# A hybrid RWKV-7 / S5 layer: the w_ada column sums as matmuls, and triangular inverses built from 16-blocks

## Chip, cores, metric

The kernel runs on one core of a Trainium2 chip. The metric is the device time of one execution in microseconds (us), lower is better. Engines are named as in the profile: PE (TensorE matmuls), PEld (its weight loads), DVE (VectorE), ACT (ScalarE), POOL (GpSimd), SP (the engine whose queue issues nearly all DMAs).

## The reference

One layer on a sequence of 1024 tokens with 1024 features, all in float32. What matters here:

```python
c_act = jax.nn.silu(c)                       # c: (1, 1024)
ada = c_act @ w_ada[l] + b_ada[l]            # w_ada: (1024, 6144), 24 MB
sh_m, sc_m, g_m, sh_f, sc_f, g_f = jnp.split(ada, 6, axis=-1)
h = modulate(rms_norm(x), sh_m, sc_m)        # parts 0 and 1 of ada
proj = h @ w_in[l]
...                                          # RWKV-7 time mixing (8 heads) and S5 state space
x = x + g_m * mix                            # part 2
h = modulate(rms_norm(x), sh_f, sc_f)        # parts 3 and 4
x = x + g_f * ffn                            # part 5
```

The RWKV recurrence `S = S * w_t + sa b_t + v_t k_t` is computed in chunks of 64 tokens. Each chunk and head needs the inverse of a unit triangular 64x64 matrix; with 1024 tokens (16 chunks) and 8 heads there are 128 such matrices.

## The kernel before

The program is a set of Python generators that are woven together; from what they yield, the framework's scheduler orders each engine's instructions by a simulated time line (`schedule_with_timeline_sim=True` at the launch), and allots tile buffers and PSUM banks. On the chip each engine then works its own queue in that order.

**The w_ada sums.** `ada_load` (L280) loads a slab of w_ada for one part and `n` column blocks of 128 in four DMAs on SP's queue; each fills a tile `wada` [128, 2, 128n]. `ada_acc` (L289) makes `acc` [128, 128n]: eight terms, w_ada rows times the column `cact[:, k]` of silu(c), added up on DVE (L295, L297), or, where `eng` is not DVE, scaled on ACT (L299) and added on POOL (L300). `ada_cols` (L303) sums `acc` over the partitions with one matmul per column block against a column of ones (tile `pac`, L306) and adds the bias into `mod` (L307). Parts 0 and 1 are done in the start (L538 to L566) with n=4, two loads of both parts; parts 2 and 3 by `ada_steps` (L826) as `adg` (L1250) beside the end of the chunk chains and the S5 gate (`s5_glu`); parts 4 and 5 as `adl` (L1428) beside the first half of the output projection. These steps have n=2 and four `wada` buffers, so one step's load waits for the one before to be read. `adg` gives the steps j=0 and j=4 of each part to ACT and POOL. The PSUM tile of `ada_cols` comes from `ps_s` in `adg` and from `ps_a` in `adl`, banks that the S5 gate and the preparation of the chunks use as well.

**The inverses.** The sequence is worked in four quarters `qt` of 256 tokens; each has 32 matrices. `amats` (L953) writes the chunk matrices to `ak`; `l_write` (L984) puts the 64x64 triangles in DRAM (`l_d`). `solve` (L991) loads the two 32x32 diagonal blocks of each matrix with one row of `LU` per partition (64 matrices, split in two column halves over 128 partitions), and runs forward substitution over 31 columns, two instructions per column (L1006, L1008), on DVE for quarters 0 and 1 and on POOL for 2 and 3. The inverse X and its transpose VT go through DRAM (`x_d`, L1010, L1011) and come back in matmul layout (`XB`, `VB`, L1020, L1021). `rest` (L1013) builds the off-diagonal 32x32 block from two rounds of 32 small matmuls (`pG`, L1028; `pO`, L1038) with an ACT copy between, and writes the result over `ak`. The chunk chains (`chunk`, L1048) of that quarter need it.

**Order around it.** Quarters 0 and 1 run beside the S5 units and the z projection (`zhalf`). Quarters 2 and 3 are the generator `late` (L1421), which runs `alongside` the first half of the FFN `f0` (L1442): matmuls of the FFN (`mm3`, L270) fill TensorE between its steps. PSUM banks come from `ps_t` by tag; `ps_g` has one bank "g" and, in part of the program, a second one "G".

Of the kernel before, what the change touches and what calls it, by code (L numbers as in the profile page):

```python
# [9 lines left out]
F32 = mybir.dt.float32  # L10
# [7 lines left out]
P = 128  # L18
D = 1024
T = 1024  # L20
HT = 512
# [8 lines left out]
def kernel(  # L30
# [127 lines left out]
    for b in range(4):  # L158
        V.memset(rm[32 * b:32 * b + 32, b % 2:b % 2 + 1], 1.0)
    m01 = const.tile([P, HT], F32, name="m01")  # L160
# [52 lines left out]
    def col(name, i=0, n=1):  # L213
        gi, o = off[name]
        return cols[:, gi, o + i:o + i + n]

    cact = const.tile([P, 8], F32, name="cact")
    nkk = const.tile([P, 4], F32, name="nkk")
# [22 lines left out]
    x_d = dram.tile([4, 2, 65536], F32, name="x_d")  # L241
# [47 lines left out]
    def ada_acc(pl, wts, n, eng=V):  # L289

        acc = pl.tile([P, 128 * n], F32, tag="acc", bufs=2 if n > 2 else 3, name="acc")
        for k in range(8):
            wt = wts[k // 2][:, k % 2, :]
            if k == 0:
                V.tensor_scalar_mul(acc, wt, cact[:, 0:1])  # L295
            elif eng is V:
                V.scalar_tensor_tensor(out=acc, in0=wt, scalar=cact[:, k:k + 1], in1=acc, op0=ALU.mult, op1=ALU.add)  # L297
            else:
                S.mul(wt, wt, cact[:, k:k + 1])  # L299
                G.tensor_tensor(out=acc, in0=acc, in1=wt, op=ALU.add)  # L300
        return acc
# [16 lines left out]
    V.tensor_mul(cact, cact, col("c", 0, 8))  # L318
    def load_x(hf):
# [220 lines left out]
    acs = [ada_acc(sp, w, 4) for w in wa]  # L540
# [12 lines left out]
    acs = [ada_acc(sp, w, 4) for w in wa]  # L553
# [122 lines left out]

    s5_params(*s5q)
# [148 lines left out]
    def ada_steps(pl, parts, ps, mix=lambda j: j % 4):  # L826

        todo = []
        def cols():
            acc, part, j = todo.pop(0)  # L830
            ada_cols(acc, part, j, 2, ps("pac2")[:, 0:2])
        for part in parts:
            for j in (0, 2, 4, 6):
                todo.append((ada_acc(pl, ada_load(pl, part, j, 2, 4), 2, V if mix(j) else None), part, j))
                if len(todo) > 2:
                    cols()
                yield
        while todo:
            cols()
            yield  # L840
# [150 lines left out]
    def solve(qt):  # L991

        t_ = lambda nm, sh: RP[0].tile(sh, F32, tag=nm, name=nm)
        LU, tmp = t_("LU", [P, 32, 32]), t_("stmp", [P, 256])
        X, VT = (RP[0].tile([P, HT], F32, tag=nm, name=nm) for nm in ("XU", "VT"))
        X, VT = X.rearrange("p (i k) -> p i k", k=16), VT.rearrange("p (k i) -> p k i", i=32)
        for o in range(2):
            nc.sync.dma_start(LU[64 * o:64 * o + 64], l_d[qt][:, 0:2048].rearrange("r (i t) -> r i t", t=64)[:, :, 0:32])
        G.memset(X, 0.0)
        for o in range(2):  # L1000
            G.memset(X[64 * o:64 * o + 64].rearrange("p i k -> p (i k)")[:, 16 * o:512:33], 1.0)
# [7 lines left out]
        SOLVE.tensor_copy(VT.rearrange("p k i -> p i k"), X)  # L1009
        nc.sync.dma_start(x_d[qt, 0].rearrange("(r n) -> r n", r=P), X.rearrange("p i k -> p (i k)"))  # L1010
        nc.sync.dma_start(x_d[qt, 1].rearrange("(r n) -> r n", r=P), VT.rearrange("p k i -> p (k i)"))  # L1011

    def rest(qt):  # L1013

        XB, VB, GT = (t.rearrange("p (u k) -> p u k", k=32) for t in
                      [RP[0].tile([P, HT], F32, tag=nm, name=nm) for nm in ("XU", "VT")] + [tr("GT")])

        for o in range(2):
            src = x_d[qt, :, 32768 * o:32768 * o + 32768]
            nc.sync.dma_start(XB[:, :, 16 * o:16 * o + 16], src[0].rearrange("(u p k) -> p u k", u=16, k=16))  # L1020
            nc.sync.dma_start(VB[o::2], src[1].rearrange("(u p i) -> p u i", u=16, i=32))  # L1021
        aks = [sts[qt, q]["ak"] for q in range(2)]
# [7 lines left out]
        for h2 in range(2):  # L1030
            p0 = 64 * h2 + 32
            S.copy(GT[p0:p0 + 32].rearrange("p u (k o) -> p u o k", o=2),
                   ps[p0:p0 + 32].rearrange("p u (o k) -> p u o k", o=2))
# [394 lines left out]
    adl = ada_steps(pool("adp3", stack=das, side="right"), (4, 5), ps_a, lambda j: True)  # L1428
# [62 lines left out]
```

## Time and profile before

| | us |
|---|---|
| median of 3 runs | 1596.32 |
| lowest and highest run | 1594.2, 1597.29 |
| the profiled execution | 1596.48 |
| its span, first to last instruction | 1594.8 |

| engine | busy us | share of the span |
|---|---|---|
| PE | 1419.0 | 89% |
| PEld | 1143.2 | 72% |
| DVE | 929.3 | 58% |
| ACT | 562.7 | 35% |
| POOL | 519.8 | 33% |

All durations below are of the profiled execution, in us from the start of its span. A busy share is a mean over stages with different limits; PEclk is the clock that TensorE was granted, as a share of 2.4 GHz, and a record is one instruction in the trace. One float32 matmul of the program leaves two records. In a row of a time line, the bracket at the end is the idle time of the engine just before the row and what ended it.

### The profile page before, as it was taken

The page shows a single profiled execution, that of the slowest core. Times are in us where ns is not written, and L with a number is a line of the kernel's source. Part 1 is how long each engine was busy: PE and PEld are TensorE (multiplying, and loading weights), DVE is VectorE, ACT ScalarE, POOL GpSimd, SP SyncE. Part 2 cuts the span into 40 slices and gives each one's busy share as a digit, 9 for nine tenths or more (in the row PEclk, how much of TensorE's full clock was granted, in tenths as well). Part 3 has the DMA queues.
Part 4 walks back from the last instruction along what each step waited for, and adds up shares of the span by engine and source line. Part 5 has one row for each costly group of instructions (what it writes and reads, how often), then busy time and mean ns, then how long its engine had stood idle before and what let it go on. Part 6 is the DMA issues. An engine that isn't in the chain of part 4 may idle for free.

```text
span 1594.8 us, 23226 instructions
## 1 busy us (share of the span) xinstructions
PE 1419.0 (89%) x9167; PEld 1143.2 (72%) x9167; DVE 929.3 (58%) x1618; ACT 562.7 (35%) x909; POOL 519.8 (33%) x480
## 2 busy tenths in 40 slices
PE   3897888988968847989999998999997999999997
PEld 3675666776856535777777776778886888888885
DVE  5968328688656899464467655446356533333335
ACT  4442244443345632242145223224444222222223
POOL 4358333222143415163000007000611244444543
PEclk9998899899979869899999999899998999999999
DMA  9447895563664477244233243315621423232331
GB/s 286 139 139 244 264 328 193 164 163 110 154 160 125 126 219 217 59 103 97 61 99 91 88 106 89 84 54 167 177 80 40 151 87 106 92 106 92 98 101 53
DMA packets 255692, 211.80 MB, mean 133 GB/s; under 512 B 71894, under 2 KB 223072, under 8 KB 252000
## 3 DMA queue, kind: packets, MB, share of 16 engines
q1 hardware_dynamic: 254096, 208.67, 44.0%
q8 instruction: 72, 1.18, 0.3%
q0 software_dynamic: 816, 0.57, 0.2%
q10 hardware_dynamic: 672, 1.08, 0.2%
q14 instruction: 36, 0.29, 0.1%
HBM read 166.54 MB, written 45.84 MB: 133 GB/s over the span
## 4 chain that ended last, share of the span: by engine, by line
PE 51%; DVE 19%; DMA 13%; POOL 5%; ACT 5%; issue 4%; SPq 2%; DVEq 0%; ACTq 0%; POOLq 0%
PE pdn L270 11%; PE pgate L270 10%; PE pup L270 10%; PE pz L270 5%; PE po L1314 4%; DMA wada<-in_w_ada_dram 3%; PE pu L367 2%; DMA rawd<-in_ffn_w_down_dram 2%; PE p L1062 2%; DVE acc L297 2%; POOL stmp L1006 2%; POOL XU L1008 2%; PE pY L762 1%; PE pA L962 1%; DMA LU<-l_d 1%
## 5 line engine op out<-in xcount | busy, mean ns | idle before, releaser
L270 PE MATMUL pdn<-wd,act 128*128 128x512 f32 x1056 | 271.7, 398 | 1.4 <-DVE x L1363 0.5
L270 PE MATMUL pup<-h,hl_up 128*128 128x512 f32 x1056 | 266.5, 395 | 0.2 <-ACT hl_up L131 0.2
L270 PE MATMUL pgate<-h,hl_g 128*128 128x512 f32 x1056 | 262.7, 394 | 2.1 <-ACT hl_g L131 2.0
L270 PEld LDWEIGHTS pdn<-wd,act 128*128 128x128 f32 x1056 | 197.3, 189 | 49.1 <-DVE x L1363 2.4
L270 PEld LDWEIGHTS pgate<-h,hl_g 128*128 128x128 f32 x1056 | 196.6, 188 | 47.2 <-issue 3.2
L270 PEld LDWEIGHTS pup<-h,hl_up 128*128 128x128 f32 x1056 | 197.5, 188 | 43.9 <-issue 2.1
L270 PE MATMUL pz<-hT,hl_z 128*128 128x256 f32 (+1 forms) x1008 | 192.6, 347 | 35.0 <-ACT zo L872 13.5
L1363 DVE TENSOR_TENSOR x<-pdn,x 128x512 f32<-128x512 f32 x176 | 118.8, 688 | 176.6 <-PE pdn L270 176.4
L270 PEld LDWEIGHTS pz<-hT,hl_z 128*128 128x128 f32 x1008 | 159.0, 206 | 64.8 <-ACT zo L872 18.2
L1398 DVE TENSOR_TENSOR rawd<-rawd,gfb 128x1024 f32<-128x1024 f32 x44 | 57.2, 1300 | 111.5 <-DMA rawd<-in_ffn_w_down_dram 89.9
L1314 PE MATMUL po<-wo,yhl 128*128 128x512 f32 x384 | 98.7, 410 | 9.0 <-ACT yhl L1299 4.2
L1314 PEld LDWEIGHTS po<-wo,yhl 128*128 128x128 f32 x384 | 74.4, 197 | 27.3 <-ACT yhl L1299 4.3
L131 ACT CAST wd<-rawd 128x1024 fp32r<-128x1024 f32 x44 | 45.6, 1051 | 122.1 <-DVE rawd L1398 88.8
L131 ACT CAST hl_up<-raw_up 128x1024 fp32r<-128x1024 f32 x44 | 46.2, 1051 | 114.6 <-PE pup L270 105.1
L297 DVE SCALAR_TENSOR_TENSOR acc<-wada,cact,acc 128x256 f32<-128x256 f32 (+1 forms) x112 | 79.0, 710 | 6.9 <-DMA wada<-in_w_ada_dram 5.3
L875 POOL TENSOR_TENSOR zo<-zo,zm 128x512 f32<-128x512 f32 x28 | 44.2, 1580 | 99.5 <-ACT zo L872 86.6
L127 POOL TENSOR_TENSOR hl_g<-raw_g,hl_g 128x1024 fp32r<-128x1024 f32 x19 | 45.5, 2394 | 78.7 <-ACT hl_g L131 78.7
L127 POOL TENSOR_TENSOR yhl<-yt,yhl 128x512 fp32r<-128x512 f32 x16 | 25.0, 1562 | 135.5 <-ACT yhl L1299 130.9
L1392 ACT ACTIVATE sgt<-pgate 128x512 f32<-128x512 f32 x44 | 26.3, 599 | 121.0 <-PE pgate L270 120.0
L127 POOL TENSOR_TENSOR wd<-rawd,wd 128x1024 fp32r<-128x1024 f32 x19 | 49.7, 2616 | 57.4 <-ACT wd L131 57.4
L127 POOL TENSOR_TENSOR wo<-wraw,wo 128x512 fp32r<-128x512 f32 x32 | 44.4, 1393 | 73.6 <-ACT wo L131 73.6
L127 POOL TENSOR_TENSOR hl_up<-raw_up,hl_up 128x1024 fp32r<-128x1024 f32 x19 | 49.9, 2628 | 50.0 <-ACT hl_up L131 50.0
(373 smaller groups left out, 2345.5 us busy)
## 6 DMA issues: line engine op xcount, KB each, us to landing
raw_g<-in_ffn_w_gate_dram SPq DMA_DIRECT2D x44, 512.0 KB, 4.0
raw_up<-in_ffn_w_up_dram SPq DMA_DIRECT2D x44, 512.0 KB, 3.9
rawd<-in_ffn_w_down_dram SPq DMA_DIRECT2D x44, 512.0 KB, 3.6
wada<-in_w_ada_dram SPq DMA_DIRECT2D x64, 256.0 KB, 3.2
zw_d<-hl_z SPq DMA_DIRECT2D x14, 1024.0 KB
hl_z<-zw_d SPq DMA_DIRECT2D x14, 1024.0 KB, 4.9
wada<-in_w_ada_dram SPq DMA_DIRECT2D x16, 512.0 KB, 7.8
wraw<-in_w_out_dram SPq DMA_DIRECT2D x32, 256.0 KB, 4.4
```

Of the source, the lines that this page charges most:

```text
L127: (eng or G).tensor_tensor(out=out, in0=a, in1=b, op=ALU.subtract)
L131: S.copy(dst[:, 0], src)
L270: PE.matmul(ps, lhsT=lf(a, k), rhs=rf(b, k), start=(n == 0), stop=(n == 3 * kb - 1))
L297: V.scalar_tensor_tensor(out=acc, in0=wt, scalar=cact[:, k:k + 1], in1=acc, op0=ALU.mult, op1=ALU.add)
L367: PE.matmul(pu[hf, b], lhsT=uw[b][:, a_, k, :], rhs=hT[hf, k][:, b_, :], start=(k == 0 and n == 0), stop=(k == 7 and n == 2))
L875: G.tensor_tensor(out=o, in0=o, in1=zm[:, 0:HT], op=ALU.add)
L1006: SOLVE.tensor_tensor(out=t, in0=LU[:, j, j + 1:32].unsqueeze(2).to_broadcast([P, nt, nk]), in1=X[:, j:j + 1, 0:nk].to_broadcast([P, nt, n ...
L1008: SOLVE.tensor_tensor(out=X[:, j + 1:32, 0:nk], in0=X[:, j + 1:32, 0:nk], in1=t, op=ALU.add)
L1062: PE.matmul(ps[r, h], lhsT=a, rhs=b, start=(n == 0), stop=(n == len(ops) - 1))
L1314: PE.matmul(pss[i], lhsT=yh[k][:, a, 128 * i:128 * i + 128], rhs=wo[:, b], start=(k == 4 and n == 0), stop=(k == 3 and n == 2))
L1363: V.tensor_tensor(out=t, in0=ps, in1=t, op=ALU.add)
L1398: V.tensor_tensor(out=raw, in0=raw, in1=gfb, op=ALU.mult)
```

## The change

Two edits come together.

1. `ada_acc` makes its sums on TensorE. A tile `cz` [128, 8, 32] is zero but for column 0 of each k, which is silu(c). For each k one matmul has `cz[:, k, :]` (128 rows, 32 columns) as the stationary side and the w_ada slab as the moving side; k modulo 4 chooses one of four column groups of the array, so four sums run in four groups of 32 output partitions, in two rounds. ACT copies the PSUM tile `pada` to `acc`; `ada_cols` is unchanged. `ada_steps` loads with eight `wada` buffers instead of four, one step ahead of the sum. `acc` has two buffers. The DVE form and the ACT and POOL form go.
2. `solve` substitutes only in the 16x16 diagonal blocks (128 of them, one per partition): 15 columns, 30 instructions, on DVE for every quarter. `rest` then builds each 32x32 diagonal inverse by three rounds of 64 matmuls of 32x32 (`pH`, `pX`, `pV`), each followed by a DVE operation of 128x512, before the two old rounds. `x_d` is one buffer for all quarters, zeroed once by two DMAs on POOL's queue.

```diff
-    def ada_acc(pl, wts, n, eng=V):
-        acc = pl.tile([P, 128 * n], F32, tag="acc", bufs=2 if n > 2 else 3, name="acc")
+    def ada_acc(pl, wts, n, ps):
         for k in range(8):
-            wt = wts[k // 2][:, k % 2, :]
-            if k == 0:
-                V.tensor_scalar_mul(acc, wt, cact[:, 0:1])
-            elif eng is V:
-                V.scalar_tensor_tensor(out=acc, in0=wt, scalar=cact[:, k:k + 1], in1=acc, op0=ALU.mult, op1=ALU.add)
-            else:
-                S.mul(wt, wt, cact[:, k:k + 1])
-                G.tensor_tensor(out=acc, in0=acc, in1=wt, op=ALU.add)
+            g = slice(32 * (k % 4), 32 * (k % 4) + 32)
+            PE.matmul(ps[g, 0:128 * n], lhsT=cz[:, k, :], rhs=wts[k // 2][:, k % 2, :], start=(k < 4), stop=(k > 3),
+                      tile_position=(0, 32 * (k % 4)))
+        acc = pl.tile([P, 128 * n], F32, tag="acc", bufs=2, name="acc")
+        S.copy(acc, ps[:, 0:128 * n])
         return acc
...
-    acs = [ada_acc(sp, w, 4) for w in wa]
+    acs = [ada_acc(sp, w, 4, pst.tile([P, 512], F32, tag="tp", bufs=3, name="pada")) for w in wa]
...
+    def ada_steps(pl, parts, ps):
+        loads, todo = [], []
+        def acc():
+            w, part, j = loads.pop(0)
+            todo.append((ada_acc(pl, w, 2, ps("pada")), part, j))
...
+                loads.append((ada_load(pl, part, j, 2, 8), part, j))
+                if len(todo) > 0:
+                    cols()
+                if len(loads) > 1:
+                    acc()
                 yield
...
     def solve(qt):
-        SOLVE = V if qt < 2 else G
-        for j in range(31):
-            nt, nk = 31 - j, j // 2 + 1
+        for j in range(15):
+            nt, nk = 15 - j, j + 1
             t = tmp[:, 0:nt * nk].rearrange("p (a b) -> p a b", b=nk)
-            SOLVE.tensor_tensor(out=t, in0=LU[:, j, j + 1:32].unsqueeze(2).to_broadcast([P, nt, nk]),
-                                in1=X[:, j:j + 1, 0:nk].to_broadcast([P, nt, nk]), op=ALU.mult)
-            SOLVE.tensor_tensor(out=X[:, j + 1:32, 0:nk], in0=X[:, j + 1:32, 0:nk], in1=t, op=ALU.add)
+            V.tensor_tensor(out=t, in0=LU[:, j, j + 1:16].unsqueeze(2).to_broadcast([P, nt, nk]),
+                            in1=X[:, j:j + 1, 0:nk].to_broadcast([P, nt, nk]), op=ALU.mult)
+            V.tensor_tensor(out=X[:, j + 1:16, 0:nk], in0=X[:, j + 1:16, 0:nk], in1=t, op=ALU.add)
...
+        for n, w in enumerate((X, VT)):
+            d = x_d[n].rearrange("(r s) (i k) -> s r i k", s=2, k=32)
+            for s_ in range(2):
+                nc.sync.dma_start(d[s_, :, :, 16 * s_:16 * s_ + 16], w[s_::2])
...
     def rest(qt):
+        def blocks(nm, lf, rf):
+            ps = ps_g(nm).rearrange("p (u k) -> p u k", k=32)
+            for u in range(16):
+                for b in range(4):
+                    r = slice(32 * b, 32 * b + 32)
+                    PE.matmul(ps[r, u, :], lhsT=lf(r, u, b), rhs=rf(r, u), start=True, stop=True,
+                              tile_position=(32 * b, 32 * b))
+            return ps
+        ps = blocks("pH", lambda r, u, b: aks[u // 8][r, u % 8, 0, 0, 32 * (b % 2):32 * (b % 2) + 32], lambda r, u: XB[r, u, :])
+        V.tensor_tensor(out=GT, in0=ps, in1=mlow.unsqueeze(1).to_broadcast([P, 16, 32]), op=ALU.mult)
+        ps = blocks("pX", lambda r, u, b: VB[r, u, :], lambda r, u: GT[r, u, :])
+        V.tensor_tensor(out=XB, in0=ps, in1=XB, op=ALU.add)
+        ps = blocks("pV", lambda r, u, b: GT[r, u, :], lambda r, u: VB[r, u, :])
+        V.tensor_tensor(out=VB, in0=ps, in1=VB, op=ALU.add)
```

## Rows read from the trace of the kernel before

**Rows 1.** Busy time of each engine, granted clock, DMA by stretch (windows view)

```profile
core 0: us, PE busy (x) PEld busy (x) DVE busy (x) ACT busy (x) POOL busy (x), PEclk, DMA share, GB/s
0.00:110.00 110.00, 76.34 (x383) 64.20 (x384) 75.75 (x207) 48.21 (x71) 43.46 (x46) 0.94 0.65 202
335.00:405.00 70.00, 62.38 (x479) 51.66 (x480) 60.54 (x144) 26.76 (x52) 15.41 (x14) 0.95 0.47 141
405.00:470.00 65.00, 54.74 (x888) 48.27 (x886) 33.68 (x116) 24.14 (x61) 16.69 (x26) 0.89 0.63 154
470.00:570.00 100.00, 79.55 (x860) 61.84 (x859) 81.69 (x180) 60.15 (x120) 40.53 (x46) 0.88 0.41 123
570.00:650.00 80.00, 52.91 (x198) 39.52 (x199) 66.36 (x116) 21.46 (x36) 33.33 (x24) 0.79 0.69 209
...
700.00:940.00 240.00, 234.98 (x1605) 181.98 (x1604) 144.26 (x218) 82.30 (x114) 31.43 (x63) 0.99 0.32 90
```

**Rows 2.** Tile acc alone, by stretch: PE, PEld, DVE, POOL busy, clock, DMA

```profile
0.00:110.00 110.00, 3.79 (x32) 4.04 (x32) 25.76 (x32) 0.00 (x0) 0.94 0.65 202
470.00:570.00 100.00, 4.11 (x28) 3.73 (x28) 22.16 (x35) 20.64 (x24) 0.88 0.41 123
570.00:650.00 80.00, 5.97 (x36) 5.67 (x36) 42.83 (x64) 0.00 (x0) 0.79 0.69 209
```

**Rows 3.** PE's waits, 570 to 650: who for whom, us, times, longest

```profile
PE pac L306 <- DVE acc L297: 5.4, 3, 2.4
```

**Rows 4.** PE's time line, 60 to 104: start, us, instruction, count

```profile
60.88 14.99 PE L367 MATMUL pu<-hT,hl_u 128*128 128x512 f32 x54 [4.26 <-DVE hT L127]
75.71 0.94 PE L306 MATMUL pac<-ones,acc 128*128 128x1 f32 x8
...
77.76 25.50 PE L367 MATMUL pu<-hT,hl_u 128*128 128x512 f32 x108 [0.52 <-ACT hT L351]
```

**Rows 5.** PE's time line: full array, two column groups, four column groups

```profile
255.55 0.71 PE L762 MATMUL pY<-L,CA 64*128 64x128 f32 x4
256.19 0.49 PE L759 MATMUL pY<-X,Tt 128*128 128x128 f32 x2
...
235.49 1.09 PE L722 MATMUL pL<-X,Bt 128*64 128x128 f32 x14
...
158.06 1.97 PE L635 MATMUL pk<-s5ca,bb 64*16 64x128 f32 x64
```

**Rows 6.** PE's time line around 412: 128x128 work, 32x32 tiles, 128x128 work

```profile
411.83 0.76 PE L270 MATMUL pz<-hT,hl_z 128*128 128x256 f32 x5
412.52 1.20 PE L1028 MATMUL pG<-XU,ak 32*32 32x32 f32 x64
413.65 0.62 PE L270 MATMUL pz<-hT,hl_z 128*128 128x256 f32 x3
```

**Rows 7.** PE's time line: the pG round of quarters 1 and 3

```profile
455.66 1.92 PE L1028 MATMUL pG<-XU,ak 32*32 32x32 f32 x64 [3.84 <-DMA XU<-x_d]
...
997.42 1.92 PE L1028 MATMUL pG<-XU,ak 32*32 32x32 f32 x64 [5.79 <-DMA XU<-x_d]
```

**Rows 8.** Tile stmp alone, by stretch: DVE busy, POOL busy, clock, DMA

```profile
405.00:450.00 45.00, 17.76 (x64) 0.00 (x0) 1.00 0.55 138
...
650.00:760.00 110.00, 0.00 (x0) 29.56 (x62) 0.95 0.40 96
```

**Rows 9.** DVE's time line: the first half of a step of the substitution

```profile
445.88 0.21 DVE L1006 TENSOR_TENSOR stmp<-LU,XU 128x45 f32<-128x45 f32 x1
```

**Rows 10.** One line each of tile pA, and of ACT's time line

```profile
L964 DVE TENSOR_TENSOR ak<-pA,mask x32: 675/688/692, 270.5 to 944.7; 128x512 f32<-128x512 f32 x32
...
566.38 0.47 ACT L804 ACTIVATE sg<-pglu,hbg 128x256 f32<-128x256 f32 x1 [2.03 <-PE pglu L270]
```

**Rows 11.** DMA issues of the page: count, KB each, us to landing

```profile
x_d<-XU SPq DMA_DIRECT2D x4, 256.0 KB, 2.0
...
XU<-x_d SPq DMA_DIRECT2D x8, 128.0 KB, 3.7
```

More of the change, by code (lines that the diff above doesn't have):

```diff
@@ L159 @@
         V.memset(rm[32 * b:32 * b + 32, b % 2:b % 2 + 1], 1.0)
+    mlow = const.tile([P, 32], F32, name="mlow")
+    V.memset(mlow, 0.0)
+    for b in range(4):
+        G.affine_select(
+            out=mlow[32 * b:32 * b + 32, 0:16], in_=mlow[32 * b:32 * b + 32, 0:16], pattern=[[0, 16]], base=16,
+            channel_multiplier=-1, compare_op=ALU.is_gt, fill=1.0,
+        )
     m01 = const.tile([P, HT], F32, name="m01")
@@ L217 @@
     cact = const.tile([P, 8], F32, name="cact")
+    cz = const.tile([P, 8, 32], F32, name="cz")
     nkk = const.tile([P, 4], F32, name="nkk")
@@ L240 @@
     l_d = dram.tile([4, 64, 2080], F32, name="l_d")
-    x_d = dram.tile([4, 2, 65536], F32, name="x_d")
+    x_d = dram.tile([2, P, HT], F32, name="x_d")
     def rsqrt_col(dst, ssum, n, eps, tmp):
@@ L552 @@
     dgs = norm_x(1, xts[1])
-    acs = [ada_acc(sp, w, 4) for w in wa]
+    acs = [ada_acc(sp, w, 4, pst.tile([P, 512], F32, tag="tp", bufs=3, name="pada")) for w in wa]
     transpose_x(xts[1], dgs)
@@ L675, in s5_params @@
                 nc.sync.dma_start(C_d[2 * Q + ri], ca[:, ri, 8 * Q:8 * Q + 8].rearrange("p g n c -> p (g n c)"))
+    zero = pp.tile([P, HT], F32, name="zero")
+    G.memset(zero, 0.0)
+    for n in range(2):
+        nc.gpsimd.dma_start(x_d[n], zero)
     s5_params(*s5q)
@@ L823, in s5_glu @@
             yield
-    def ada_steps(pl, parts, ps, mix=lambda j: j % 4):
-        todo = []
+    def ada_steps(pl, parts, ps):
[3 more added lines that the diff above has]
+            todo.append((ada_acc(pl, w, 2, ps("pada")), part, j))
         def cols():
-            acc, part, j = todo.pop(0)
-            ada_cols(acc, part, j, 2, ps("pac2")[:, 0:2])
+            a, part, j = todo.pop(0)
+            ada_cols(a, part, j, 2, ps("pac2")[:, 0:2])
         for part in parts:
             for j in (0, 2, 4, 6):
-                todo.append((ada_acc(pl, ada_load(pl, part, j, 2, 4), 2, V if mix(j) else None), part, j))
-                if len(todo) > 2:
+                loads.append((ada_load(pl, part, j, 2, 8), part, j))
+                if len(todo) > 0:
                     cols()
+                if len(loads) > 1:
+                    acc()
                 yield
-        while todo:
-            cols()
+        while loads or todo:
+            if todo:
+                cols()
+            if loads:
+                acc()
             yield
@@ L1010, in solve @@
-        nc.sync.dma_start(x_d[qt, 0].rearrange("(r n) -> r n", r=P), X.rearrange("p i k -> p (i k)"))
-        nc.sync.dma_start(x_d[qt, 1].rearrange("(r n) -> r n", r=P), VT.rearrange("p k i -> p (k i)"))
-    def rest(qt):
[L1015 to L1021, printed above, removed]
-        aks = [sts[qt, q]["ak"] for q in range(2)]
+        LU, tmp, X, VT = t_("LU", [P, 16, 16]), t_("stmp", [P, 64]), t_("X16", [P, 16, 16]), t_("V16", [P, 16, 16])
@@ L1031, in rest @@
             p0 = 64 * h2 + 32
[L1032 to L1033 removed]
+            S.copy(GT[p0:p0 + 32], ps[p0:p0 + 32])
         ps = ps_g("pO").rearrange("p (u k) -> p u k", k=32)
```

22 lines of the change are left out of this document (13 added, 9 removed).

## The prediction

> **What bounds the kernel now.** I read the busy times by stretch first [rows 1], then the instructions of one tile at a time, then time lines where an engine stood still. Time counts as the profiled execution's, 1596.48 us, 0.16 us above the median of the runs, so nothing is converted. From 700 to 940 PE is busy 235.0 of 240 us at 0.99 of full clock [rows 1]: there only matmul time counts, and a faster DVE or POOL buys nothing. The first 700 us are otherwise. PE has 33.7 us free in 0 to 110, 7.6 in 335 to 405, 10.3 in 405 to 470, 20.5 in 470 to 570 and 27.1 in 570 to 650, there at a clock of 0.79 [rows 1]. In the last two DVE is the fullest engine (81.7 of 100, 66.4 of 80), and the rows of tile `acc` show with what: the sums of w_ada and their small `mod` operations hold DVE for 25.8, 22.2 and 42.8 us in three stretches, and POOL for 20.6 in one [rows 2]. In 570 to 650 PE waits 5.4 us for these sums directly [rows 3]; the rest of their harm is that everything else on DVE's queue stands behind them.
>
> **What the sums cost on PE.** One n=2 step is 8 float32 matmuls of 256 columns, so 16 records. Whether four column groups really run at once decides their price. With the whole array in use, 4 records of 128 columns take 0.71 us and 2 take 0.49 [rows 5]: 0.11 us for one more. In two column groups 14 take 1.09 us, 0.078 each; in four, 64 take 1.97 us, 0.031 each [rows 5], 3.6 times denser. At 256 columns these are 0.22, 0.16 and 0.062 us, so a step costs 3.5, 2.5 or 1.0 us, and an n=4 step twice that. Over 16 and 4 steps: 84, 60 or 24 us. I take 24, the row with four groups, since the change uses four. That row has 64 rows of the array and 16 columns, the change 128 and 32, so the upper ends stay in the range.
> The Trainium skill (TensorE: Matmul & The Clock Gate, Part 3, measured speedup) gives 2.38 times for three column groups; as an estimate by that page a step would cost 1.5 us and all sums 35, 11 more than in my sum. The four-group row of this case is denser than that.
>
> **Start, 0 to 110: -4 us, from -9 to +4.** w_ada and x must first land: the DMA share is 0.65 over the whole stretch [rows 1], and nothing in the change loads less. What can go is PE's 4.26 us wait behind DVE before 60.88, and the slow pace after it (54 matmuls in 14.99 us, 0.278 each, against 0.236 for the 108 that follow, 54 x 0.042 = 2.2 us [rows 4]). Of these 6.5 us I take back 2.5: of the second pair of n=4 steps, 2.0 us each, a part falls into the very wait that goes. The four ACT copies and the first pair lie in PE's free time; the two DVE operations that fill `cz` ahead of the first sum run while the slabs are still landing, at no cost but the first sum's start. The mods wait in PE's queue anyway: `pac` at 75.71 stands behind the 54 matmuls [rows 4]. Against it: `pada` takes its banks from the three that the transposes use. If that holds them up for one DMA it costs 4 us, my upper end.
>
> **Inverses of quarters 0 and 1, 335 to 470: +1 us, from -8 to +9.** Removed on DVE: 17.8 us a quarter [rows 8]. Added: 30 operations of 14 to 64 columns at about the 0.21 us of one with 45 [rows 9], 6 us; three of 128x512 at 0.69 [rows 10], 2.1 us; a copy, 0.3. DVE gains 9.4 us a quarter. Added on PE: three rounds of 64 matmuls, 128 records each. 64 records of 32x32 take 1.20 us at full clock [rows 6], so up to 2.4 us a round, or 2.1 if the 0.27 us that a row spends beyond its pace (0.71 - 4 x 0.11 [rows 5]) is paid once; 6.3 to 7.2 a quarter, 13 us for two. Of PE's 17.9 us free [rows 1] I let the shorter solve give back 12: the 3.84 us before `pG` [rows 7], its cold clock (1.92 instead of 1.20 us), and about half the rest, since SP's queue, which holds the reload of the inverse and the gate's loads behind it, moves on earlier. If none comes back it is +9 (some rounds lie in waits anyway), if all, -8. The DMAs: `LU` has half the bytes, the inverse is written in 64-byte pieces instead of whole rows. Writing took 2.0 us, reading 16-wide pieces 3.7 [rows 11]; I price the write at either (0 to +2 us a quarter, in the latency only) and take the upper one. `x_d` is now one buffer, so a quarter's write waits for the reload of the quarter before; a whole chunk chain lies between, cost nothing. The zeroing on POOL's queue lies over 200 us before its first reader; cost nothing, at worst its two issues.
>
> **Sums of parts 2 to 5, 470 to 650: -21 us, from -38 to -4.** In 470 to 570 DVE loses 22 of 82 us, POOL 20.6 and ACT as many scalings; added are 8 ACT copies of 0.47 [rows 10] and 8 us on PE, which has 20.5 free. The chunk chains, the gate and the next preparation share this stretch and have waits of their own, on tables and on each other, so I count only -6 (from -13 to +4). In 570 to 650 DVE loses 42.8 of 66.4 us. PE's own work is 52.9 us, some at half clock, and 8 are added; the DMAs' is 0.69 of 80, 55 us [rows 1]. Both put the floor near 60. Five of the 20 I leave to SP's order and to the banks: -15 (from -25 to 0). With eight buffers the loads no longer wait for DVE to read the step before. A new wait stands on PE's queue: a sum whose slab has not landed holds whatever stands behind it, chain and gate matmuls alike, where today DVE's queue was held. The cover is the load one step ahead; if it is gone, the step pays its landing.
>
> **Inverses of quarters 2 and 3, from 700: +7 us, from 0 to +16.** Here the 29.6 us of POOL a quarter [rows 8] were off the critical path: PE was full beside them. What is removed is worth only the 5.79 us wait for `XU` at 997 [rows 7]. What is added is 13 us of matmuls (2 times 6.3 to 7.2) on the engine that sets the time. 13 - 6 is +7. Should the reload be late as before, +13, and +16 with a second such wait in part; should the scheduler find free slots for half the rounds, 0.
>
> **Sum.** -4 + 1 - 21 + 7 = -17, so 1596.5 - 17 = 1579.5 us. The change pays in the first 650 us and charges in the FFN.
>
> **Rivals.**
> (a) DVE was all that held 470 to 650. Then PE closes its whole 47.6 us less the 16 added, and the clock's loss of about 10 comes back: -42 instead of -21, 1558 us. For it: DVE is the fullest engine in both stretches. Against: 55 us of DMA in the second.
> (b) The banks become the bound. `pada` comes from the same single bank as `pac`, the gate and the preparation. It is held from the first matmul through ACT's copy: about 1.0 + 0.47 us and ACT's queue before it, in all 1.5 to 2 us more a step, 16 steps, up to 28 us in stretches that gain 21 otherwise. It decides once other users of the bank already stand in line. With a quarter of the steps free it is 21 us, the gain of these stretches is gone, and the sum is -4 + 1 + 0 + 7: 1600 us; with half of them free, 1593. Taken at 1597, no change.
> (c) Slower: the rounds of quarters 2 and 3 stall PE. Each of the five rounds needs the result of DVE or ACT on the round before, on one bank; if the order puts no FFN matmul between them, each of the three new hand-overs costs a DVE operation (0.69 [rows 10]) plus what stands before it on DVE, some 2 us. A quarter then costs 7 us of matmuls, 6 of hand-overs and, for quarter 2 as for quarter 3 today, a late reload of 5.8 [rows 7]: 2 x 13 + 5.8 = 32 us instead of 7, the sum is -4 + 1 - 21 + 32 = +8, 1604.5 us. It decides once PE has nothing queued between the rounds. Against: PE is 98% busy from 700 to 940, a quarter's small rounds among them [rows 1].
> (d) The column groups don't run at once with 128 rows: 60 us more on PE (84 - 24). PE's free time takes some 30 of it: -17 + 30 is 1610 us. The row with four groups speaks against it [rows 5].
> (e) In the trace a 128x128 round ended at 412.59, the 32x32 round began at 412.52 and the next 128x128 round at 413.65, before its 1.20 us were over [rows 6]: changing the shape cost nothing to be seen. Priced by the latency that one round shows beyond its pace (the 0.27 us above), 64 changes of shape, two for each of 20 sums and 12 rounds, would make 17 us, and the sum 1597 us. The Trainium skill (TensorEngine Tiling (Array Packing), Key Properties) says that a change of tiling mode drains TensorE; it gives no figure, and the rows of this case show no such gap.
>
> **How the numbers follow.** The forecast 0.52, (a) 0.14, (b) 0.11, (c) 0.13, (d) 0.06, (e) 0.04. The likelier halves of the terms' bounds make the forecast 1564 to 1591 by itself. The range for 8 in 10 takes in the price of (a) with the start's lower end, and (c) with a little more: 1552 to 1606. It leaves out (d), the worse half of (c) and the far end of (a). This kernel's measurement tells apart about 0.2%, 3.2 us: faster is under 1593.3, slower over 1599.7. Faster has the forecast, (a) and a little of (b): 0.68. Within: most of (b) and (e), 0.11. Slower: (c), (d) and the rest, 0.21.
>
> **What would show it.** Right: no `acc` on DVE or POOL; `pada` records at about 62 ns of 256 columns, DVE under 50 us in the 80 us after 570; the FFN's start some 22 us earlier; after it PE just as full, with 12 to 14 us of `pH`, `pX`, `pV` in all for quarters 2 and 3. Wrong: `pada` records at 0.2 us (d); PE waiting on the copy of `pada` or for w_ada (b); PE idle between `pH` and `pG` late in the run (c); or a start that gets longer because the transposes wait for banks.

## The result and the profile after

| | before | after |
|---|---|---|
| median of 7 runs, us | 1597.29 | 1612.9 |
| lowest and highest | 1594.2, 1603.87 | 1607.39, 1618.94 |
| the profiled execution and its span | 1596.48, 1594.8 | 1618.94, 1617.2 |

The ratio is 1.0095, with 1.0066 to 1.0124 as its 95% interval: the change makes the kernel slower by some 15 us. The forecast was 1579.5 and faster. The profiled execution of after is the slowest of its seven, so its stages are read against each other and not to the last microsecond.

Busy time by stretch, of after, beside [rows 1] (columns as there):

```profile
core 0: us, PE busy (x) PEld busy (x) DVE busy (x) ACT busy (x) POOL busy (x), PEclk, DMA share, GB/s
0.00:110.00 110.00, 92.21 (x444) 63.67 (x445) 51.49 (x177) 51.66 (x75) 42.59 (x53) 1.00 0.66 202
335.00:405.00 70.00, 61.16 (x524) 51.08 (x526) 56.50 (x124) 26.14 (x48) 16.87 (x17) 0.85 0.54 144
405.00:470.00 65.00, 60.32 (x1282) 54.66 (x1283) 24.75 (x76) 15.01 (x39) 6.17 (x9) 0.92 0.39 102
470.00:570.00 100.00, 85.99 (x1295) 66.01 (x1294) 55.72 (x134) 55.02 (x109) 26.09 (x31) 0.95 0.50 154
570.00:650.00 80.00, 62.01 (x263) 42.72 (x265) 44.60 (x69) 33.30 (x59) 30.99 (x24) 0.77 0.54 161
...
700.00:940.00 240.00, 238.71 (x1986) 189.03 (x1987) 152.87 (x257) 85.65 (x124) 9.07 (x9) 0.99 0.32 90
```

The change does what it says: DVE falls from 81.7 to 55.7 us and from 66.4 to 44.6 in the two stretches of the sums, and POOL does 9.1 us of work in 700 to 940 where it did 31.4. But these stretches didn't get shorter by that. In after the gate starts at 482 us and the FFN at 709; in before at 462 and 694. So 20 us are lost ahead of the gate, 5 are won back between gate and FFN (227 us in place of 232), and the output ends at 1613 in place of 1591: 7 more are lost in the FFN. Of the 20, 7 are there at quarter 0's first `l_d` (290.7 in place of 283.4), before any inverse is worked. The FFN up to the end of the output projection takes 508 us in place of 510; it is the stretch after that which is longer, 400 us in place of 391. These are readings of single traces. `p1_128` and `p2_32` below have one order and, but for where their tiles lie, the same work, and their traces still part by 5 us at quarter 0's first `l_d` and by 9 at the FFN's start, so a stage difference of that size is not shown by traces alone.

The sums' price on PE, tile `pada` in after's time line:

```profile
38.15 1.05 PE L303 MATMUL pada<-wada,cz 128*32 128x512 f32 x4
...
529.88 1.07 PE L303 MATMUL pada<-wada,cz 128*32 128x256 f32 x16
```

and its busy time by stretch:

```profile
0.00:110.00 110.00, 19.14 (x64) 2.43 (x64) 2.35 (x4) 1.00 0.66 202
470.00:600.00 130.00, 13.65 (x144) 4.12 (x144) 3.29 (x9) 0.88 0.52 160
600.00:700.00 100.00, 11.90 (x112) 3.77 (x112) 2.58 (x7) 0.83 0.46 142
```

Late in the run 16 records of 256 columns take 1.07 us, 67 ns each: four column groups at once, as forecast. In the start the same 1.05 us go to 4 records of 512 columns, half as dense, because a slab has only two of the eight k and each sum runs as its slabs land: two groups at work. Sixteen such pieces, the first ones at half clock, make 19.1 us where I had 8.

### The profile page after: what moved, and what is told of

Same layout as the page of the kernel before. It is cut to its first block, busy times and chain, and to the rows that moved or that the text cites. A ratio compares the mean times of both kernels' runs of the same rounds, so it can differ in the third digit from the quotient of the medians.

```text
span 1617.2 us, 26606 instructions
## 1 busy us (share of the span) xinstructions
PE 1481.3 (92%) x11023; PEld 1170.1 (72%) x11023; DVE 859.4 (53%) x1499; ACT 561.4 (35%) x903; POOL 429.4 (27%) x329
## 4 chain that ended last, share of the span: by engine, by line
PE 68%; DVE 13%; DMA 9%; ACT 4%; issue 4%; SPq 2%; POOL 1%; DVEq 0%; ACTq 0%; POOLq 0%
PE pgate L280 14%; PE pup L280 13%; PE pdn L280 13%; PE pz L280 5%; PE po L1347 4%; PE p L1095 3%; PE pu L375 3%; PE pada L303 2%; PE pA L982 2%; PE pY L774 2%; DMA wada<-in_w_ada_dram 1%; PE ptr L1373 1%; DMA yt<-y_d 1%; PE ptr L352 1%; DMA rawd<-in_ffn_w_down_dram 1%
## 5 line engine op out<-in xcount | busy, mean ns | idle before, releaser
L280 PEld LDWEIGHTS pz<-hT,hl_z 128*128 128x128 f32 x1008 | 164.6, 215 | 48.7 <-DVE hl_z L127 10.7
L1347 PE MATMUL po<-wo,yhl 128*128 128x512 f32 x384 | 94.7, 401 | 1.7 <-POOL wo L127 1.1
L891 ACT ACTIVATE zm<-pz,cols 128x256 f32<-128x256 f32 (+1 forms) x42 | 22.9, 544 | 118.2 <-PE pz L280 118.0
L303 PE MATMUL pada<-wada,cz 128*32 128x256 f32 (+1 forms) x320 | 44.7, 508 | 17.7 <-DMA wada<-in_w_ada_dram 8.7
```

The lines of the kernel that those rows point to most:

```text
L280: PE.matmul(ps, lhsT=lf(a, k), rhs=rf(b, k), start=(n == 0), stop=(n == 3 * kb - 1))
L303: PE.matmul(ps[g, 0:128 * n], lhsT=cz[:, k, :], rhs=wts[k // 2][:, k % 2, :], start=(k < 4), stop=(k > 3), tile_position=(0, 32 * (k % 4)))
L1347: PE.matmul(pss[i], lhsT=yh[k][:, a, 128 * i:128 * i + 128], rhs=wo[:, b], start=(k == 4 and n == 0), stop=(k == 3 and n == 2))
```

## The experiments

**First four: one part of the change at a time, and none of it.** `e1_ada` has the sums alone, `e2_solve` the inverses alone, `e3_norounds` the inverses without the rounds, `e4_null` only what is unused:

```diff
+    mlow = const.tile([P, 32], F32, name="mlow")     # filled as in the change
+    cz = const.tile([P, 8, 32], F32, name="cz")      # filled as in the change
+    n_d = dram.tile([2, P, HT], F32, name="n_d")
...
+        nc.gpsimd.dma_start(n_d[n], zero)
```

> The kernel before with the w_ada sums on TensorE alone; the inverses stay as before, by substitution over 32 rows, on VectorE and GpSimd. Theory (the inverses lost the time): against the kernel before -8 to 0 us, the modulation sums of parts 2 to 5 giving some 5 to 8 us in the stretch from 470 to 650, the start nothing. Rival 1 (the sums lost it: some 45 us more work on a TensorE that is over 90% busy in the start, and a chain over one PSUM bank at the end of parts 4 and 5): +8 to +15 us, of which +4 to +8 by the time of the first LU write of quarter 0. Rival 2 (neither part, but the order that the instructions fall into): e1 and e2 each move by a few us at places where nothing was changed, and their differences from before don't add up to that of the changed kernel (+15).

> The kernel before with the inverses by substitution in 16-blocks alone; the w_ada sums stay on VectorE (and GpSimd). Theory: against the kernel before +12 to +18 us, the last PE work of quarter 1's inverse (pO) some 10 us later than in the kernel before (463) although its substitution ends some 20 us earlier, and +5 to +9 more where quarters 2 and 3 pass. Rival 1 (the sums lost it): -3 to +4 us, pO of quarter 1 at most 3 us later. Rival 2 (order): anything within +-10, with shifts before 335 us, where this kernel does nothing else than the one before but two writes of zeros.

> As e2_solve, without the three rounds of small matmuls (pH, pX, pV) and the three VectorE operations between them in every quarter: the blocks of 16 below the diagonal stay zero in the inverse of each 32-block, so that part of the computation is left out. Theory (the added hand-overs lose what the shorter substitution gains): -6 to +1 us against the kernel before, that is 14 to 20 under e2_solve, although the rounds' own work is only some 7 us a quarter. If the rounds cost no more than their own instructions on TensorE (3 x 1.7 us a quarter), the difference to e2_solve is 4 to 8 us in total. If the loss lies elsewhere (sums, order): within 4 us of e2_solve.

> The kernel before with what computes nothing that is used: the constant masks mlow and cz, the zero tile, and two GpSimd transfers of zeros to a new place in DRAM. Theory: within 2 us of the kernel before, milestones before 335 us within 1 us. Rival (the order noise of an inert edit): a shift of 4 to 8 us, already there at the first write of quarter 0's triangular blocks (283 before, 291 in the changed kernel).

| run | median, us | ratio to before |
|---|---|---|
| `e1_ada` | 1581.5 | 0.991 (0.988 to 0.994) |
| `e2_solve` | 1631.4 | 1.021 (1.018 to 1.024) |
| `e3_norounds` | 1596.6 | 0.999 (0.998 to 1.001) |
| `e4_null` | 1623.4 | 1.017 (1.014 to 1.020) |

The inverses lose 34 us, twice what I expected, the sums gain 15, again more than expected, and the two add up to the changed kernel within 5 us. Without the rounds nothing is lost. So far the theory holds by its signs. But fourteen instructions that compute nothing used cost 27 us, more than the whole change. No difference between two of these kernels could be trusted until that was understood.

**Order held.** The framework's scheduler orders every engine's queue anew for each kernel. In the kernels whose names begin with h, the instructions that two kernels share stand, engine by engine, in the order of one of them; what only one has goes where the scheduler puts it. Each has this, with a list `order` of its own:

```diff
+    info = mybir.DependencyInfo(mybir.DependencyClass.NoSync, mybir.DependencyReason.DATA)
+    for places in order.values():          # one list for each engine
+        for a, b in zip(places, places[1:]):
+            tc.add_manual_dep(traced[b], traced[a].name, info, reason="order")
```

> e4_null with every instruction of the kernel before held, on each engine, in the order in which the kernel before has it (dependencies of order alone between neighbours, no waits); only its 14 unused instructions stand where the scheduler puts them. Theory (the scheduler's order is what cost e4_null 27 us, not its instructions): within 3 us of the kernel before, 1593 to 1600. Rival (the unused instructions cost it themselves, the two transfers on GpSimd's queue for one): 1615 to 1625, as e4_null (1623.4).

> The counter-test: the kernel before, nothing added and nothing taken away, with its instructions held in the order that e4_null has. Theory (order): 1618 to 1626, slower than the kernel before by 20 to 30 us with the very same instructions. Rival (the unused instructions): 1594 to 1600.

> e2_solve (the inverses by 16-blocks alone; 1631.4 as the scheduler orders it) with all instructions that it shares with the kernel before held in that kernel's order; the new ones (substitution, transfers of x_d, rounds) go where the scheduler puts them between these. Theory (most of e2_solve's 34 us is order): -4 to +8 us against the kernel before, by the forecast's own terms for the inverses, +1 and +7, and the rounds measured at 1.7 us each in place of 2.1 to 2.4. Rival (the hand-overs of the three rounds cost it, order or not): +20 to +35.

> The changed kernel with all instructions that it shares with e1_ada (the sums alone, 1581.5) held in e1_ada's order. So it is e1_ada plus the new inverses, in one order. Theory (order): 1578 to 1590, faster than the kernel before by 6 to 18 us although it computes what the changed kernel (1612.9) computes. Rival (the inverses cost some 30 us in any order): 1605 to 1618.

| run | what, in whose order | median, us | ratio to before |
|---|---|---|---|
| `h1_null` | `e4_null` in that of before | 1606.2 | 1.0065 (1.0041 to 1.0089) |
| `h5_before` | before in that of `e4_null` | 1615.2 | 1.0126 (1.0099 to 1.0153) |
| `h2_solve` | `e2_solve` in that of before | 1632.2 | 1.0227 (1.0201 to 1.0253) |
| `h4_after` | the change in that of `e1_ada` | 1615.1 | 1.0125 (1.0100 to 1.0150) |

`h5_before` is the kernel before, instruction for instruction, and 20 us slower: order alone does that. `h1_null` misses what I expected by 6 us, so something is left that is neither order nor work. My theory that most of the inverses' loss was order falls with `h2_solve` and `h4_after`: they cost 36 us in before's order, 34 in their own (`e2_solve`), 34 on top of the sums in one order (`h4_after` against `e1_ada`) and 31 in free orders (the changed kernel against `e1_ada`).

Since `h2_solve` and before have one order, their time lines can be laid side by side. PE, SP and DVE around quarter 0 in `h2_solve`, in before `pG` stood at 412.5:

```profile
407.73 1.29 PE L1039 MATMUL pH<-XU,ak 32*32 32x32 f32 x128
...
410.76 1.61 PE L1039 MATMUL pX<-GT,VT 32*32 32x32 f32 x128
...
424.89 1.92 PE L1054 MATMUL pG<-XU,ak 32*32 32x32 f32 x64 [8.03 <-DVE VT L1048]
```

```profile
373.87 1.35 SPq L1022 DMA_DIRECT2D x_d<-V  x2
377.59 0.38 SPq L1030 DMA_DIRECT2D VT<-x_d  x1
403.77 0.62 SPq L1030 DMA_DIRECT2D XU<-x_d  x1
```

```profile
419.49 0.17 DVE L1014 TENSOR_TENSOR stmp<-LU,X 128x15 f32<-128x15 f32 x1 [5.19 <-DMA LU<-l_d]
...
424.15 0.69 DVE L1048 TENSOR_TENSOR VT<-pV,VT 128x512 f32<-128x512 f32 x1
```

The inverse of the 16-blocks is written at 375, 30 us ahead of before (405). Its reload `XU` leaves SP's queue at 404, behind other transfers. The three rounds then run at 408 to 417, and the last DVE operation that `pG` waits for stands in DVE's queue behind most of the substitution of quarter 1, which itself waits 5.2 us for `LU`: `pG` comes 12 us later than in before. For quarter 0 the 30 us were won on a path that had slack, and the rounds were added behind it.

In the changed kernel's own order it is quarter 1 that suffers. Its time line on PE:

```profile
447.69 0.55 PE L1047 MATMUL pH<-XU,ak 32*32 32x32 f32 x40
448.17 3.14 PE L280 MATMUL pz<-hT,hl_z 128*128 128x256 f32 x24
451.24 0.95 PE L1047 MATMUL pH<-XU,ak 32*32 32x32 f32 x88
...
456.50 0.97 PE L1047 MATMUL pX<-GT,VT 32*32 32x32 f32 x90
457.40 3.31 PE L280 MATMUL pz<-hT,hl_z 128*128 128x256 f32 x24
460.64 0.54 PE L1047 MATMUL pX<-GT,VT 32*32 32x32 f32 x38
...
466.19 0.97 PE L1047 MATMUL pV<-VT,GT 32*32 32x32 f32 x90
467.24 3.14 PE L280 MATMUL pz<-hT,hl_z 128*128 128x256 f32 x24
470.31 0.54 PE L1047 MATMUL pV<-VT,GT 32*32 32x32 f32 x38
```

Each round is cut in two by a block of the z projection, and further blocks lie between the rounds: 23 us from `pH` to the end of `pV` for 4.5 us of matmuls, so `pG` moves from 455.66 [rows 7] to 472; 8 of these 16 us were there when quarter 1's `LU` was loaded (422 in place of 414). PE is busy meanwhile (60.3 of 65 us), but with work that had no hurry; the chunk chains that wait for quarter 1 then run when that filler is used up.

**What was neither order nor work: addresses.** With one order, `h1_null` and before stay within 3 us of each other up to 1210 us, and part only then. The same FFN matmuls, by form, 1220 to 1580, in before and in `p1_128` below (busy, mean ns of one):

```profile
L270 PE MATMUL pup<-h,hl_up 128*128 128x512 f32 x524 | 128.9, 389 | 0.2 <-ACT hl_up L131 0.2
L270 PE MATMUL pgate<-h,hl_g 128*128 128x512 f32 x523 | 126.1, 390 | 1.2 <-ACT hl_g L131 1.2
```

```profile
L271 PE MATMUL pup<-h,hl_up 128*128 128x512 f32 x517 | 130.1, 395 | 0.2 <-ACT hl_up L131 0.2
L271 PE MATMUL pgate<-h,hl_g 128*128 128x512 f32 x516 | 126.8, 395 | 1.1 <-ACT hl_g L131 1.1
```

at a granted clock of 1.00 in both. What those kernels have in common is `mlow`, 128 bytes per partition, behind which all later tiles lie 128 bytes higher. `p1_128` and `p2_32` are before with an unused tile of that or a smaller size and nothing else; in `p3_after` the change's `mlow` takes 1024 bytes:

```diff
+    const.tile([P, 32], F32, name="pad")        # p1_128; [P, 8] in p2_32
...
-    mlow = const.tile([P, 32], F32, name="mlow")
+    mlow = const.tile([P, 256], F32, name="mlow")[:, 0:32]        # p3_after
```

> The kernel before with a tile of 128 bytes per partition that no instruction uses, allocated where the changed kernel allocates mlow: the same instructions in the same order, only the tiles behind it lie 128 bytes higher in SBUF (hl_up, hl_g and act of the FFN at 96 in place of 480, modulo 512 bytes). Theory (addresses): in the traces so far the matmuls of the last 360 us take 389 to 390 ns in every kernel without mlow and 393 to 396 with it, at the same granted clock, so the last stretch is 7 to 9 us longer, and the kernel 6 to 12 us slower than before. Rival (what those kernels also have in common, the added instructions or the order): within 2 us of the kernel before.

> As p1_128 with an unused tile of 32 bytes per partition (the FFN's tiles at 0 modulo 512). If only the step from 480 to 96 is bad: within 2 us of the kernel before. If every place but the old one is slower: +6 to +12 us. If a place at a multiple of 512 is better than 480: -5 to -10 us.

> The changed kernel with mlow's tile padded from 128 to 1024 bytes per partition (its 32 used columns as before), so that the FFN's tiles lie at 480 modulo 512 again; same instructions in the same order. Theory (addresses): 6 to 12 us faster than the changed kernel (1612.9), 1601 to 1607; its last stretch 391 to 394 us in place of 400. Rival: 1611 to 1615.

`p1_128` 1602.6, ratio 1.0033 (1.0006 to 1.0059); `p2_32` 1603.6, 1.0042 (1.0019 to 1.0065), its matmuls 393 to 397 ns; `p3_after` 1605.3, 1.0063 (1.0035 to 1.0091), its matmuls back at 389 to 390 ns, 8 us under the changed kernel by the medians and 5 by the ratios. So an allocation costs 5 to 8 us here. Why 480 modulo 512 is a better place for these operands than 96 or 0 stays open.

**What the rounds cost.** `h7_norounds` is `h2_solve` without them, `h8_nohand` with their matmuls but without the three DVE operations between:

```diff
-        ps = blocks("pH", ...)
-        V.tensor_tensor(out=GT, in0=ps, in1=mlow..., op=ALU.mult)
-        ps = blocks("pX", lambda r, u, b: VB[r, u, :], lambda r, u: GT[r, u, :])
-        V.tensor_tensor(out=XB, in0=ps, in1=XB, op=ALU.add)
-        ps = blocks("pV", lambda r, u, b: GT[r, u, :], lambda r, u: VB[r, u, :])
-        V.tensor_tensor(out=VB, in0=ps, in1=VB, op=ALU.add)
+        blocks("pH", ...)        # h8_nohand; h7_norounds has none of the three
+        blocks("pX", lambda r, u, b: VB[r, u, :], lambda r, u: XB[r, u, :])
+        blocks("pV", lambda r, u, b: XB[r, u, :], lambda r, u: VB[r, u, :])
```

> e3_norounds (the 16-block substitution without the three rounds and their VectorE operations; the blocks of 16 below the diagonal stay zero, part of the computation is left out) in the order of the kernel before, as h2_solve (1632.2). Theory (the rounds' hand-overs lose the time in any order, and 8 us are addresses): 1592 to 1604, so 28 to 40 us under h2_solve, for 12 rounds whose own matmuls take 1.3 to 1.9 us each. Rival (the rounds cost only their own work): 1615 to 1625.

> As h2_solve (1632.2, order of the kernel before), with the rounds' matmuls pH, pX and pV kept, all three on XB and VB as loaded, and the three VectorE operations between them left out, so that no round waits for another (the blocks of 16 below the diagonal stay zero: part of the computation is left out). h7_norounds without the matmuls is 1585.5. Theory (the hand-overs cost most of the 47 us): 1600 to 1610, that is h7 plus 12 rounds of 1.3 to 1.9 us. Rival (TensorE's own work on the rounds and what it pushes): 1620 to 1632.

`h7_norounds` 1585.5, ratio 0.9926 (0.9899 to 0.9953); `h8_nohand` 1623.9, 1.0193 (1.0149 to 1.0237); `h2_solve` was 1632.2. The rounds cost 47 us for 12 of them. I had put that down to the hand-overs, and these are 5 to 8 us of it, hardly clear of the noise (the intervals of `h8_nohand` and `h2_solve` overlap). With the hand-overs gone the matmuls alone still cost 38. And without the rounds the new substitution is 11 us faster than before, which is under my range, with the cost of `mlow`'s place in SBUF still in it. By stage, `h2_solve` and then `h7_norounds`, up to quarter 2's first `l_d` and from there to the end of the output projection:

```profile
400.00:690.00 290.00, 223.63 (x2894) 181.99 (x2889) 186.14 (x409) 112.38 (x230) 90.34 (x94) 0.82 0.46 136
690.00:1230.00 540.00, 523.90 (x4212) 415.47 (x4210) 307.71 (x507) 179.43 (x270) 45.17 (x35) 0.99 0.35 95
```

```profile
400.00:663.00 263.00, 207.94 (x2122) 167.23 (x2119) 184.87 (x401) 112.47 (x230) 93.26 (x94) 0.87 0.50 149
663.00:1183.00 520.00, 510.36 (x3439) 403.89 (x3437) 305.85 (x503) 179.03 (x270) 45.18 (x35) 1.00 0.36 98
```

Before has the same order, with these two stages:

```profile
400.00:673.00 273.00, 212.61 (x2137) 170.06 (x2132) 196.14 (x448) 112.48 (x230) 94.40 (x98) 0.86 0.53 150
673.00:1204.00 531.00, 514.06 (x3443) 407.29 (x3442) 293.31 (x441) 180.00 (x270) 108.26 (x162) 0.99 0.36 99
```

So the new substitution alone wins 10 and 11 us in the two stages, and the rounds then add 27 and 20, together the 47 of the medians. PE's busy time grows with them by 15.7 and 13.5 us, more than the rounds' own 10.0 and 8.1 (`pH`, `pX` and `pV` in these two stretches); the granted clock is lower (0.82 for 0.87, 0.99 for 1.00), so other matmuls take longer too. PE's idle time grows by 11 and 6.5. The clock and PE's waits of `h2_solve`, just behind quarter 2's rounds and from 690 to 1230:

```profile
760.00:770.00 10.00, 7.86 (x110) 6.49 (x111) 4.28 (x9) 2.61 (x4) 0.00 (x0) 0.66 0.02 3
```

```profile
PE pV L1039 <- issue: 3.1, 2, 1.6
PE pG L1054 <- DVE VT L1048: 1.6, 2, 0.8
PE pV L1039 <- DVE XU L1046: 1.6, 2, 0.8
```

Without hand-overs the idle time is partly this, `h8_nohand`:

```profile
417.35 0.63 PE L1051 MATMUL pG<-XU,ak 32*32 32x32 f32 x28
420.23 1.17 PE L1051 MATMUL pG<-XU,ak 32*32 32x32 f32 x36 [2.25 <-issue]
```

a stop within one run of matmuls, with no wait that the profile shows. Eight such stops, at the rounds and at `pG`, make 12.7 us in `h8_nohand`, six make 7.9 in `h2_solve`; before has none there. The Trainium skill (Runtime: NRT & Kernel Launch, Instruction fetch mechanics) says that engines stream their instructions in blocks and that the refills are mostly hidden. These stops aren't hidden; whether they are refills, no run here shows. In the changed kernel's own order, where z projection lies between the rounds, only 0.7 us are of this kind.

**Can the scheduler mend it?** `p4_prio` traces the rounds of `p3_after` at high priority:

```diff
+        with tc.high_priority():        # the three rounds and their DVE operations inside
```

> p3_after (the changed kernel with mlow padded, 1605.3) with the three rounds and their VectorE operations traced under the scheduler's high priority, so that they stand ahead of the z projection and the FFN in TensorE's queue once their operands are there. Theory (in the changed kernel's own order the rounds of quarter 1 stretch over 27 us because blocks of the z projection stand between them): pG of quarter 1 at 455 to 462 in place of 470, and 1590 to 1600 us in all. Rival (the waits between rounds are then paid on TensorE in place of filler work): 1603 to 1612.

1602.8, ratio 1.0064 (1.0034 to 1.0095), as `p3_after`; `pG` of quarter 1 came at 468, not at 455 to 462. The time is at the rival's lower end. But blocks of the z projection still stand between the rounds of quarter 1 (at 451.67, 458.02 and 464.60), so the edit didn't bring about the order that it was to try, and that no order is better is not shown.

**The sums, with order held outside the stretches they change.** `h3_ada` is `e1_ada`, `h9_late` the same with the start left on DVE; `e5_late` is `h9_late` in a free order, `h6_after` the whole change held like `h3_ada`:

```diff
-    acs = [ada_acc(sp, w, 4, pst.tile([P, 512], F32, tag="tp", bufs=3, name="pada")) for w in wa]
+    acs = [ada_acc_v(sp, w, 4) for w in wa]        # h9_late, e5_late: the DVE form of before
```

> e1_ada (the sums alone, 1581.5) with the order of the kernel before held for everything but the start (ahead of the first pz) and the generators woven between the first and the last w_ada step of parts 2 to 5. Theory (the sums themselves gain): -16 to -8 us against the kernel before, as e1_ada. Rival (e1_ada's gain is mostly its order): -6 to +4 us.

> As h3_ada, with the sums of parts 0 and 1 in the start left on VectorE as in the kernel before; the start is then in the order of before too. Theory (in the start the sums on TensorE gain nothing, since TensorE is full there: pz began at 105 us in before and in the changed kernel): within 4 us of h3_ada. The forecast's own term for the start would make it 4 us slower than h3_ada; if TensorE's 19 us of sums in the start are paid in full it is 8 to 19 us faster.

> The changed kernel with what it shares with the kernel before held in that kernel's order, but for the start and the stretch of the w_ada steps of parts 2 to 5 (as h3_ada). Theory (the parts' costs in this order add up, and the changed kernel's own order gives them back in part): 1596 + 10 (h3_ada) + 36 (h2_solve) = 1642, 1632 to 1650. Rival (order matters little for the two together): 1608 to 1618, as the changed kernel.

> The sums on TensorE for parts 2 to 5 alone, the start and the inverses as in the kernel before, in the order that the scheduler gives. h9_late is the same with the order of before outside that stretch (1590.8). If the order changes little: 1586 to 1596. If the new order gains as much as e1_ada's did against h3_ada (24 us): 1565 to 1575. If it loses as e4_null's did: 1605 to 1615.

| run | median, us | ratio to before |
|---|---|---|
| `h3_ada` | 1605.3 | 1.0061 (1.0035 to 1.0087) |
| `h9_late` | 1590.8 | 0.9979 (0.9951 to 1.0008) |
| `h6_after` | 1637.4 | 1.0270 (1.0242 to 1.0298) |
| `e5_late` | 1596.2 | 1.0001 (0.9975 to 1.0028) |

In one order the parts add up: +10 and +36 give 46, and `h6_after` has +43. The changed kernel as scheduled has +15, so its own order gives some 25 to 28 us back; `e1_ada` is 24 us better in its own order than `h3_ada`. The later sums alone are worth 3 to 5 us in before's order, not clear of the noise, and nothing in a free one. `h3_ada` loses more than even the rival had. It is 14.5 us behind `h9_late`, where I had expected 4 at most; in the traces 6 are there at 400 us (`l_d` at 407 against 401), 9 when the output projection ends (653 against 644), 18 at the FFN's start (703 against 685). The last nine come at the end of the w_ada steps, where order was free. The 6 us ahead of that are no more than two traces of one order can part by, and the start's order was free too: whether the start's sums lose them is not shown.

## Why the prediction was wrong

**Inverses of quarters 0 and 1: forecast +1, measured +17** (`h2_solve`, first `l_d` of quarter 2 at 690 for 673). This is the step that failed most, and in it the price of the rounds: 13 us of matmuls on PE and nothing beside them. The 12 us that I let the shorter substitution give back came in the main: without the rounds (`h7_norounds`) the same `l_d` is at 663, 10 us ahead of before, and over the whole run that kernel is 11 us faster in spite of 5 to 8 us by address, 16 to 19 for the 12 and 6 that I had. With them it is at 690, so they cost 27 us. Their own matmuls are 10.0 of these, 1.3 to 1.9 us a round and less than the 2.1 to 2.4 that I had; some 6 (15.7 less 10.0) go with the lower clock, and 11 are idle time of PE, which holds the 8.0 us that `pG` waits behind quarter 1's substitution and the stops without a wait. Clock and idle time I had put at nothing. Why matmuls without hand-overs bring so much of both stays open. The bounds were wrong by themselves: +9 lies under the full price of 13, and 13 less all 17.9 us of free time is -5, not -8.

**Inverses of quarters 2 and 3: forecast +7, measured +9** (531 us in before, 540 in `h2_solve`). That the number is near is luck: both its terms were too small. The substitution and its late reload were worth 11 us (531 to 520 in `h7_norounds`) where I had 6, and the rounds cost 20 where I had 13: 8.1 of their own, some 5 with the clock (13.5 less 8.1), 6.5 idle. Rival (c) had the right sign, `pH` to `pG` takes 11 us in `h2_solve` for quarter 2, but the waits for DVE's hand-overs are 3.2 us in all and not its 12. In the changed kernel's own order neither shows: there PE is busy for 238.7 of 240 us, and the FFN takes 508 us up to the end of the output projection, 2 less than in before.

**Start: forecast -4, +1 at its end.** The first `pz` begins at 105.28 in after, 104.38 in before. The failed step is the 2.0 us for an n=4 sum: it needs all four groups, and slabs that land one by one fill two. PE gets 19.1 us instead of 8 and is full from 60 us on. Some 6 us more are lost up to quarter 0's first `l_d`, but `e2_solve` and `e4_null`, without these sums, come there as late (290.4 and 290.3), so the sums aren't shown to lose them.

**Sums of parts 2 to 5: forecast -21, measured -3 to -5** in before's order (`h9_late`, not clear of the noise); in its trace the FFN starts 9 us earlier than in before's. Gate to FFN, before and `h9_late`:

```profile
462.00:694.00 232.00, 175.56 (x1410) 137.01 (x1410) 174.62 (x342) 103.11 (x200) 92.45 (x88) 0.85 0.50 147
```

```profile
461.00:685.00 224.00, 189.72 (x1667) 139.59 (x1668) 118.25 (x243) 96.31 (x188) 66.97 (x60) 0.88 0.50 153
```

DVE has 56 us less, PE 14 more. PE's idle time falls by 22 us, from 56 to 34, and 14 of these go to its own new work; I had wanted 37 (21 and the 16 added). The sums' price was right (16 steps, 21.7 us with some at half clock, where I had 16), their share in what held the stretch was not: freeing DVE gave back 22 us of PE's idle time, not 37. (The rows of tile `acc` hold the sums alone, 8 operations each, and not the `mod` operations.) What is late next is a chain of small waits, none over 5 us in sum in `h9_late`. In after the longest is the one that the forecast named, a sum that holds PE's queue until its slab lands (482 to 709):

```profile
PE pada L303 <- DMA wada<-in_w_ada_dram: 7.7, 3, 4.8
```

The last part of that stretch in after is the one bank of rival (b):

```profile
671.42 1.94 PE L303 MATMUL pada<-wada,cz 128*32 128x256 f32 x16 [0.25 <-DVE mod L313]
673.88 1.01 PE L312 MATMUL pac<-ones,acc 128*128 128x1 f32 x4 [0.52 <-ACT acc L306]
675.14 1.94 PE L303 MATMUL pada<-wada,cz 128*32 128x256 f32 x16 [0.25 <-DVE mod L313]
```

Sum, copy, `pac` and `mod` one after the other, 3.7 us a step at half clock, after the output projection has ended at 667. In before the last `pac` came at 645, 18 us ahead of its end (664).

**Not in the forecast: 5 to 8 us by address, and order.** In sum, the inverses came to +31 to +36 in four pairs of kernels for my +8, addresses among it, and the sums as scheduled to -15 or -18 (`e1_ada`; the change against `e2_solve`) for my -25: some 26 and 8 of the 33 us between forecast and result. How much of the changed kernel's own figure is its order can be bounded only by these pairs: 20 us lost in `e4_null`, 24 won in `e1_ada`.

**The rivals.** (a) fell: DVE was not all that held the stretch. (b) holds for the last steps, and in the waits for slabs. (c) is answered above. (d) and (e) fell: 67 ns a record, and in after's rows above the z projection begins at 448.17 while the round before it ends at 448.24. The Trainium skill (TensorEngine Tiling (Array Packing), Key Properties) says that a change of tiling mode drains TensorE; this trace shows no gap for it.

**A version faster than both** is `e1_ada`: the sums on TensorE, the inverses as before, 1581.5. Its gain belongs to that kernel as scheduled; in before's order the same edit loses.

## What to carry to other kernels

Before an edit is priced by its instructions, run the kernel with something inert in its place: here that moved the time by 27 us, more than either part of the change was meant to. Where a scheduler writes the order, hold the order of the old kernel by order-only dependencies and pad the new tiles, and the parts of an edit become measurable; here they then added up to within 3 us. A step made shorter is worth what its reader's queue can take earlier: look where the transfer and the next instruction stand on their engines. And price small matmuls on the fullest engine by a run with and a run without them: here 18 us of them cost 47.

## What the runs showed of the hardware

The same float32 matmul of 128x512 took 389 to 390 ns with its operands at 480 modulo 512 bytes in SBUF, 393 to 396 at 96 and 393 to 397 at 0, all at full clock. A stream of 32x32 matmuls stopped, with no wait in the trace, for up to 2.5 us at a time, 12.7 us in all in `h8_nohand`. Four column groups of 128 rows ran at once, 16 records of 256 columns in 1.07 us. 128 records of 32x32 in four positions took 1.29 us.
